# RWKV's 64x64 blocks all turned by products with the identity, none in TensorE's transpose mode

## The chip, the cores and the metric

The kernel runs on one core of one Trainium2 chip. The metric is device time in microseconds (us) of one execution, lower is better. The engines named are TensorE (PE, with its weight loads PEld), VectorE (DVE), ScalarE (ACT), GpSimd (POOL) and SyncE (SP, which issues most DMAs).

## What is computed

One inference step of a two-layer decoder for 256 prompt positions and 8 sample rows, so that each activation tile has 264 columns. Layer 0 runs an RWKV-7 mixer and an S5 mixer side by side, layer 1 a retention mixer; each layer ends with a SwiGLU FFN. The part that this change touches is RWKV's recurrence over the prompt, for 16 heads of width 64:

```python
def step(S, inp):
    r_t, w_t, k_t, v_t, kk_t, a_t = inp
    sa = jnp.einsum('bhij,bhj->bhi', S, kk_t)
    S = (S * w_t[:, :, None, :] - sa[..., None] * (kk_t * a_t)[:, :, None, :]
         + v_t[..., None] * k_t[:, :, None, :])
    return S, jnp.einsum('bhij,bhj->bhi', S, r_t)
```

The kernel computes it in 4 chunks of 64 positions for a pair of heads at a time. In that form blocks of 64x64 (values, scores, and matrices of a step-wise inversion) are needed turned, rows for columns.

## The kernel before

All weights stream from HBM in loads of 512 KB. ACT rounds each 128x512 piece to `wh`, DVE forms the rest `wl`, and PE multiplies three times (`xh,wh`, `xl,wh`, `xh,wl`) for float32 accuracy. `run_stream` writes these stream products in one fixed order: layer 0's input projection, a GLU, its output projection, the FFN, then layer 1.

RWKV, S5 and the eight sample rows are side work. Each is a generator that records operations; `pump` puts recorded operations between stream products, at most 3.3 us of PE work by its own count for a set of four weight blocks in layer 0. What is ready is judged by a planner's clocks: `emit` adds the price of each operation from `cost`. No wait that the chip really has comes back into it, and on each engine the instructions then run in exactly the order written. For PE the prices (us, at full clock; doubled when the planner thinks the clock low) of the 64x64 work are:

```python
            if name == "transpose":
                return 0.11 if w > 64 else 0.04
            if w <= 32:
                return max(0.034, 0.02 + 0.42e-3 * n)
            if w <= 64:
                return max(0.08, 1.05e-3 * n)
```

RWKV's prompt part handles head pairs p = 0 to 7. `front(p)` prepares a pair and `back(p)` does the chunked recurrence. `HS` are the two halves of the 128 partitions, one head in each, `NC_` is 4 chunks, `id2` an identity in each half. `turned` turns one block. It is called in four groups for each pair: in `front` eight times for the values `xv` (from one half into the other), and in `back`, at level 0, eight times for the scores `at`, six times for `AR` (chunks 1 to 3) and eight times for `Ym`. Within a group the output goes to the upper and the lower half in turn. In the trace a block in transpose mode leaves one MATMUL record, a float32 product leaves two.

The sample rows (`rwkv_sample_half`) matter because they wait for DMAs. For each of the eight pairs DVE multiplies a product with `bones` (a 128x512 multiply that reads `ps`), POOL subtracts, a DMA spreads a row over 64 partitions, and then DVE multiplies again, `self.mul(t, t, vb("k"))`, a 128x512 multiply that waits for that DMA. All that stands behind it on DVE waits with it, the `wl` pieces of the stream too.

Of the kernel before, what the change touches and what calls it, by code (L numbers as in the profile page):

```python
# [41 lines left out]
FAR = 1 << 20  # L42
# [85 lines left out]
class Builder:  # L128
# [271 lines left out]

    def turned(self, out, a, one):

        if out.offset % FAR < out.ap[0][0]:
            self.P.transpose(out, a, one)
        else:
            self.P.matmul(out, a, one, start=True, stop=True)

    def gcopy(self, out, a):
        self.G.tensor_scalar(out, a, 1.0, None, op0=OP.mult)
# [1399 lines left out]
```

## Time and profile before

| what | value |
|---|---|
| median of 3 runs (lowest, highest) | 3212.47 us (3202.04, 3217.61) |
| the profiled execution's own time | 3204.68 us |
| its span, first to last instruction | 3202.9 us |
| busy PE, DVE, ACT, POOL | 3121.3 us, 1972.0 us, 1498.7 us, 343.4 us |
| mean granted TensorE clock | 0.981 |
| first load of FFN weights issued at | 719.2 us |

RWKV's prompt part, where the change lies, runs between some 80 and 650 us from the span's start; behind it PE runs stream products almost without a gap. A MATMUL record's length is not what it costs, since records overlap; what counts is the distance from one start to the next.

### The profile page before, as it was taken

How to read it: one execution, taken by the hardware profiler on the slowest of the kernel's cores; microseconds unless marked ns; L12 is line 12 of the kernel's file. 1: busy time of each engine (PE TensorE's matmuls, PEld its weight loads, DVE VectorE, ACT ScalarE, POOL GpSimd, SP SyncE). 2: the span in 40 equal slices, each digit the busy share in tenths (PEclk: the TensorE clock that was granted, in tenths of full speed). 3: DMA queues.
4: the chain of work that ended last, by engine and by line, in shares of the span. 5: the costliest groups of instructions: out<-in, count | busy, mean ns of one | idle time of the engine just before them, and what ended most of it. 6: DMA issues, size and time to landing. Idle time of an engine off the chain costs nothing.

```text
span 3202.9 us, 65844 instructions
## 1 busy us (share of the span) xinstructions
PE 3121.3 (97%) x26390; PEld 2967.3 (93%) x26390; DVE 1972.0 (62%) x3702; ACT 1498.7 (47%) x2733; POOL 343.4 (11%) x525
## 2 busy tenths in 40 slices
PE   7999798899999999999999999999999999999998
PEld 7987687799999999999998998988899999999998
DVE  6788666466555555566566666565566565555554
ACT  6543355255444444455344444444455444444454
POOL 5111332100000000001111111011100000000001
PEclk9999899799999999999999999999999999999999
DMA  5323413455655556666666677567666555565654
GB/s 192 120 86 74 61 54 70 84 163 183 179 184 180 182 179 184 181 182 211 216 230 219 230 250 254 174 244 250 217 179 184 181 182 184 178 183 180 184 179 152
DMA packets 161138, 560.54 MB, mean 175 GB/s; under 512 B 21312, under 2 KB 23744, under 8 KB 160576
## 3 DMA queue, kind: packets, MB, share of 16 engines
q1 hardware_dynamic: 140384, 483.29, 50.7%
q0 software_dynamic: 19584, 71.31, 5.9%
q8 instruction: 207, 3.39, 0.4%
q10 hardware_dynamic: 864, 1.74, 0.1%
q14 instruction: 99, 0.81, 0.1%
HBM read 511.45 MB, written 42.69 MB: 173 GB/s over the span
## 4 chain that ended last, share of the span: by engine, by line
PE 92%; DVE 3%; DMA 2%; ACT 1%; POOL 1%; issue 0%; SPq 0%; DVEq 0%; POOLq 0%; ACTq 0%
PE ps L279 92%; DMA ar_tmp<-ar_tmp 2%; DVE ar_tmp L279 1%; POOL ar_tmp L279 1%; DVE wl L279 1%; DVE t L279 1%; ACT ar_tmp L279 0%; ACT wh L279 0%; DVE ar_hidb L279 0%; DVE ar_hidy L279 0%; SPq L279 0%; DVE xl L279 0%; DVE ar_hida L279 0%; POOL ar_hida L279 0%; ACT L285 0%
## 5 line engine op out<-in xcount | busy, mean ns | idle before, releaser
L279 DVE TENSOR_TENSOR wl<-raw,wh 128x512 fp32r<-128x512 f32 x1784 | 1260.6, 710 | 904.1 <-ACT wh L279 892.5
L279 ACT ACTIVATE wh<-raw 128x512 fp32r<-128x512 f32 x1784 | 1098.9, 628 | 936.3 <-PE ps L279 905.5
L279 PE MATMUL ps<-xh,wh 128*128 128x264 f32 x4512 | 1330.0, 295 | 14.7 <-ACT wh L279 12.4
L279 PE MATMUL ps<-xh,wl 128*128 128x264 f32 x4512 | 1289.7, 286 | 10.8 <-DVE wl L279 10.7
L279 PE MATMUL ps<-xl,wh 128*128 128x264 f32 x4512 | 1287.8, 285 | 0.0
L279 PEld LDWEIGHTS ps<-xh,wh 128*128 128x128 f32 x4512 | 858.8, 190 | 63.4 <-issue 28.6
L279 PEld LDWEIGHTS ps<-xh,wl 128*128 128x128 f32 x4512 | 856.4, 190 | 12.6 <-DVE wl L279 12.6
L279 PEld LDWEIGHTS ps<-xl,wh 128*128 128x128 f32 x4512 | 860.0, 191 | 5.7 <-issue 4.8
L279 PE MATMUL ps<-hl,wh 128*128 128x264 f32 x1280 | 364.0, 284 | 0.0
L279 PE MATMUL ps<-hh,wl 128*128 128x264 f32 x1280 | 363.9, 284 | 0.0
L279 PE MATMUL ps<-hh,wh 128*128 128x264 f32 x1280 | 363.8, 284 | 0.0
L279 PE MATMUL ps<-n,wh 128*128 128x264 f32 x1408 | 257.4, 284 | 0.0
L279 PE MATMUL ps<-ar_tmp 64*64 64x64 f32 (+8 forms) x2912 | 215.3, 283 | 39.5 <-DVE ar_tmp L279 24.6
L279 PEld LDWEIGHTS ps<-hh,wh 128*128 128x128 f32 x1280 | 241.4, 189 | 0.0
L279 PEld LDWEIGHTS ps<-hl,wh 128*128 128x128 f32 x1280 | 240.9, 188 | 0.0
L279 PEld LDWEIGHTS ps<-hh,wl 128*128 128x128 f32 x1280 | 240.7, 188 | 0.0
L279 PEld LDWEIGHTS ps<-ar_tmp 64*64 64x64 f32 (+3 forms) x2912 | 149.3, 149 | 82.3 <-DVE ar_tmp L279 28.9
L279 POOL TENSOR_TENSOR sqs<-sq,sqs 128x264 f32<-128x264 f32 x56 | 42.4, 758 | 1663.5 <-ACT sq L279 1663.5
L279 PEld LDWEIGHTS ps<-n,wh 128*128 128x128 f32 x1408 | 217.8, 188 | 0.0
L279 PE MATMUL ps<-n,wl 128*128 128x264 f32 x704 | 199.6, 284 | 0.0
L279 PE MATMUL ps<-omh,wh 128*128 128x264 f32 x512 | 147.1, 287 | 0.0
L279 PE MATMUL ps<-omh,wl 128*128 128x264 f32 x512 | 145.6, 284 | 0.0
(214 smaller groups left out, 2872.1 us busy)
## 6 DMA issues: line engine op xcount, KB each, us to landing
raw<-in_w_in_c_dram SPq DMA_DIRECT2D x192, 512.0 KB, 4.3
raw<-in_ffn_w_gate_dram SPq DMA_DIRECT2D x176, 512.0 KB, 3.6
raw<-in_ffn_w_up_dram SPq DMA_DIRECT2D x176, 512.0 KB, 3.7
raw<-in_ffn_w_down_dram SPq DMA_DIRECT2D x176, 512.0 KB, 3.7
out_dram<-ar_tmp POOLq DMA_DIRECT2D x72, 512.0 KB, 4.3
raw<-in_w_in_a_dram SPq DMA_DIRECT2D x68, 512.0 KB, 3.7
ar_tmp<-in_state_ret_dram POOLq DMA_DIRECT2D x64, 512.0 KB, 6.9
raw<-in_w_out_c_dram SPq DMA_DIRECT2D x64, 512.0 KB, 3.8
```

The costliest lines, as they stand in the source:

```text
L279: getattr(eng.eng, name)(*a, **k)
```

## The change

`turned` no longer looks at where its output lies. Before, a block whose output starts at partition 0 went through `P.transpose` and one whose output starts at partition 64 through `P.matmul` with the identity; now both go through `P.matmul`. Numbers are the same up to rounding.

```diff
     def turned(self, out, a, one):
 
-        if out.offset % FAR < out.ap[0][0]:
-            self.P.transpose(out, a, one)
-        else:
-            self.P.matmul(out, a, one, start=True, stop=True)
+        self.P.matmul(out, a, one, start=True, stop=True)
```

The planner now prices such a block 0.08 instead of 0.04, so that what `pump` places around it moves. The number of instructions on each engine stays: 21546 rows on PE, 2665 rows on DVE, before and now.

On PE, at the level-0 groups of an early pair: `cst` is the identity's tile, the group of six is `AR`, the group of eight behind it is `at`, and `xh,wh` and the like are stream products. Before:

```order
L279 MATMUL ps_76<-xh,wl 128x264
L279 MATMUL ps_71<-cst,ar_hidb 128x128 x4
L279 MATMUL ps_70<-cst,ar_hidb 64x64 x6
L279 MATMUL ps_72<-cst,ar_tmp 64x64 x8
L279 MATMUL ps_76<-xh,wh 128x264
L279 MATMUL ps_76<-xl,wh 128x264
```

Now, at the same place:

```order
L279 MATMUL ps_75<-xh,wl 128x264
L279 MATMUL ps_71<-cst,ar_hidb 128x128 x4
L279 MATMUL ps_70<-cst,ar_hidb 64x64 x6
L279 MATMUL ps_72<-cst,ar_tmp 64x64 x8
L279 MATMUL ps_71<-ar_tmp 64x64 x8
L279 MATMUL ps_75<-xh,wh 128x264
```

The groups themselves stay as they are; a group of score products (`ar_tmp 64x64 x8`) now follows at once, ahead of the stream products.

On DVE, in the second half of the sample rows: the first row is the multiply of the `bones` product, the last is the multiply that waits for the DMA, `wl<-raw,wh` is a piece of the stream, the rest is RWKV's. Before, all rows between the two:

```order
L279 TENSOR_TENSOR ar_tmp<-ps_72,ar_tmp 128x512
L279 TENSOR_TENSOR wl<-raw,wh 128x512
L279 TENSOR_TENSOR ar_tmp<-ps_71,cst 128x256
L279 TENSOR_TENSOR ar_tmp<-ar_tmp,ps_70 128x256
L279 TENSOR_TENSOR ar_hidb<-t_77,ar_hida 128x4x64
L279 TENSOR_TENSOR ar_tmp<-ar_tmp,ps_72 128x256
L279 SCALAR_TENSOR_TENSOR ar_hidy<-t_77,pcol,ar_hidy 128x256
L279 TENSOR_TENSOR ar_tmp<-ar_tmp,ps_69 128x256
L279 TENSOR_TENSOR ar_hidb<-ar_hidy,ar_hida 128x4x64
L279 SCALAR_TENSOR_TENSOR ar_hidy<-t_77,pcol,ar_hida 128x256
L279 TENSOR_TENSOR ar_tmp<-ar_tmp 128x512
```

Now, the last twelve rows up to the waiting multiply (four more stand between the first multiply and these):

```order
L279 TENSOR_TENSOR ar_tmp<-ar_tmp,ps_69 128x256
L279 TENSOR_TENSOR ar_hidb<-ar_hidy,ar_hida 128x4x64
L279 TENSOR_TENSOR ar_hidb<-cst,ps_71 128x3x64
L279 SCALAR_TENSOR_TENSOR ar_hidy<-t_77,pcol,ar_hida 128x256
L279 TENSOR_TENSOR ar_hidb<-ar_hidy,ar_hida 64x4x64
L279 TENSOR_TENSOR wl<-raw,wh 128x512
L279 TENSOR_TENSOR ar_hidb<-ar_hidy,ar_hida 64x4x64
L279 TENSOR_TENSOR ar_hidb<-ar_hidb,ps_72 128x3x64
L279 TENSOR_TENSOR ar_tmp<-ps_70,ar_hidx 128x256
L279 TENSOR_TENSOR ar_tmp<-ps_69,cst 128x256
L279 TENSOR_TENSOR ar_hidb<-ps_71,t_77 128x256
L279 TENSOR_TENSOR ar_tmp<-ar_tmp 128x512
```

The waiting multiply came 10 rows after the first multiply and now comes 15 rows after it. Over the eight pairs of the sample rows these distances were 18, 13, 14, 11, 10, 8, 9 and 8 rows (91 in all) and are now 19, 14, 20, 20, 15, 9, 10 and 6 (113 in all).

## Rows read from the trace of the kernel before

**Rows 1.** The page: the chain that ended last, shares by engine.

```profile
PE 92%; DVE 3%; DMA 2%; ACT 1%; POOL 1%; issue 0%; SPq 0%; DVEq 0%; POOLq 0%; ACTq 0%
```

**Rows 2.** Busy time of each engine (instructions) in stretches from the span's start.

```profile
core 0: us, PE busy (x) PEld busy (x) DVE busy (x) ACT busy (x) POOL busy (x), PEclk, DMA share, GB/s
...
160.00:240.00 80.00, 75.20 (x761) 65.03 (x761) 67.69 (x189) 33.60 (x67) 12.97 (x25) 0.94 0.28 85
240.00:320.00 80.00, 73.61 (x834) 61.25 (x830) 67.29 (x205) 26.06 (x55) 15.52 (x23) 0.91 0.35 75
...
720.00:800.00 80.00, 79.83 (x657) 79.56 (x657) 49.52 (x85) 43.46 (x81) 3.79 (x5) 1.00 0.60 181
80.00:640.00 560.00, 510.21 (x5459) 437.61 (x5458) 392.20 (x1024) 235.79 (x518) 132.90 (x211) 0.91 0.35 78
```

**Rows 3.** Pieces of the chain: start us, us, what; xn merges n pieces.

```profile
242.20 35.31 PE ps L279 x465
...
293.02 10.07 DMA ar_tmp<-ar_tmp
...
371.75 10.56 DMA ar_tmp<-ar_tmp
...
578.78 10.08 DMA ar_tmp<-ar_tmp
```

**Rows 4.** Waits, 80 to 660 us: who <- for whom: us, times, longest.

```profile
DVE ar_tmp L279 <- DMA ar_tmp<-ar_tmp: 50.0, 8, 9.1
...
PE ps L279 <- DVE ar_tmp L279: 28.4, 12, 7.3
```

**Rows 5.** PE's timeline, one group of eight turned blocks: start us, us, xrecords.

```profile
187.05 0.24 PE L279 MATMUL ps<-cst,ar_tmp 64*64 64x64 f32 x1
...
187.22 0.27 PE L279 MATMUL ps<-cst,ar_tmp 64*64 64x64 f32 x1
...
187.05 1.78 PE L279 MATMUL ps<-cst,ar_tmp 64*64 64x64 f32 x12
188.76 0.39 PE L279 MATMUL ps<-xh,wh 128*128 128x264 f32 x1
```

**Rows 6.** PE's timeline, groups of eight and of six 64x64 products alone.

```profile
425.99 0.68 PE L279 MATMUL ps<-ar_tmp 64*64 64x64 f32 x16
426.60 0.70 PE L279 MATMUL ps<-ar_tmp,cst 128*128 128x256 f32 x2
...
259.57 0.56 PE L279 MATMUL ps<-ar_hidb,ar_tmp 64*64 64x64 f32 x12
260.07 0.72 PE L279 MATMUL ps<-ar_hidx,ar_hida 64*128 64x264 f32 x4
```

**Rows 7.** PE's timeline, a turned group in DVE's wait for a DMA.

```profile
372.37 1.78 PE L279 MATMUL ps<-cst,ar_tmp 64*64 64x64 f32 x12
```

**Rows 8.** Both kinds of group while the clock was low; windows as in rows 2.

```profile
599.88 2.64 PE L279 MATMUL ps<-cst,ar_tmp 64*64 64x64 f32 x12
602.45 1.22 PE L279 MATMUL ps<-ar_tmp,cst 128*128 128x256 f32 x2
...
304.43 1.12 PE L279 MATMUL ps<-ar_tmp 64*64 64x64 f32 x16 [5.19 <-DVE ar_tmp L279]
305.48 0.79 PE L279 MATMUL ps<-ar_hidy,cst 128*128 128x256 f32 x1
...
301.00:315.00 14.00, 10.57 (x75) 7.45 (x76) 9.66 (x25) 0.00 (x0) 4.45 (x8) 0.51 0.30 83
...
591.00:615.00 24.00, 22.65 (x181) 17.20 (x180) 10.62 (x24) 7.26 (x16) 4.71 (x5) 0.51 0.55 89
```

**Rows 9.** DVE's timeline up to a multiply that waits for its DMA.

```profile
289.28 0.68 DVE L279 TENSOR_TENSOR ar_tmp<-ps,ar_tmp 128x512 f32<-128x512 f32 x1
...
296.97 0.26 DVE L279 TENSOR_TENSOR t<-t,ar_tmp 128x64 f32<-128x64 f32 x1
303.18 0.69 DVE L279 TENSOR_TENSOR ar_tmp<-ar_tmp 128x512 f32<-128x512 f32 x1 [5.95 <-DMA ar_tmp<-ar_tmp]
```

## The prediction

> **What bounds the kernel now.** I read the chain that ended last first: 92% of it is PE, with only 3% DVE and 2% DMA [rows 1]. The table by stage then shows where that is not the whole story. From 640 us on PE has nothing to wait for (79.83 us busy in a stretch of 80), while between 80 and 640 us, the stage of RWKV's prompt part, PE is busy for 510 of 560 us at a granted clock of 0.91, and DVE comes close behind with 67.7 and 67.3 us busy in stretches of 80 [rows 2]. In this stage the chain alternates: long PE pieces such as the one of 35.31 us from 242 us, then DVE pieces, and seven DMA pieces of some 10.5 us each, of which three are shown [rows 3]. The list of waits says whose they are: DVE waits for the sample rows' DMA eight times, 50.0 us in all, and PE in turn waits 28.4 us for what DVE makes [rows 4]. So a microsecond saved on PE in this stage counts where the chain is PE, and is lost where a DMA or DVE would have come last anyway.
>
> **What a turned group costs now.** Eight blocks, four in transpose mode and four as products, leave 4 x 1 + 4 x 2 = 12 records. One such group starts at 187.05 us and the next instruction behind it at 188.76 us: 1.71 us, or 0.43 us for a pair of one transposition and one product. Within the pair the transposition's start is 0.17 us ahead of the product's first pass (187.05 to 187.22), so the product takes the other 0.26 us until the next transposition begins [rows 5]. Nothing in the group overlaps.
>
> **What it will cost.** The trace has the new form already: groups of eight float32 products of 64x64, alternating between the same two halves. Eight products are 16 records and take 425.99 to 426.60 = 0.61 us; six products are 12 records and take 259.57 to 260.07 = 0.50 us [rows 6]. More records take about a third of the time because products for the two halves run side by side. The bounds: at best 0.61 us a group, at worst, if products with the identity don't overlap, 8 x 0.26 = 2.08 us. I take 0.61 us, since shape, halves and alternation are those of the rows; `front`'s group crosses from one half to the other, which also gives two different halves in turn.
>
> There are 8 head pairs x 4 groups = 32 groups, 24 of eight blocks and 8 of six. The saving for a group of eight is 1.71 - 0.61 = 1.10 us, for one of six 3 x 0.43 - 0.50 = 0.79 us. PE's saving is 24 x 1.10 + 8 x 0.79 = 32.7 us.
>
> **What of it lies on the path.** I laid the starts of the 32 groups beside the chain's pieces. Six lie outside its PE pieces: four in DMA pieces, as the one at 372.37 us in the piece from 371.75 [rows 3, 7], and two ahead of the piece at 293 us, where DVE leads. Five are of eight blocks and one of six. The other 26 (19 and 7) save 19 x 1.10 + 7 x 0.79 = 26.4 us.
>
> Three corrections.
>
> First, the clock. In 591 to 615 us the granted clock is 0.51, the level of 1.2 GHz, after PE had stood idle in the DMA waits before it. Three groups lie there. At this level a mixed group takes 599.88 to 602.45 = 2.57 us and a group of products, in a stretch of the same clock, 304.43 to 305.48 = 1.05 us: 1.52 instead of 1.10 us saved, so 3 x 0.42 = 1.3 us more [rows 8].
>
> Second, DVE. Eleven of the 26 groups (8 and 3) start before 280 us, where DVE is busy for 67 of 80 us [rows 2]. They save 8 x 1.10 + 3 x 0.79 = 11.2 us; with PE that much quicker DVE has little slack left and will sometimes be last instead. Between nothing and all of it lost, I take half: 5.6 us.
>
> Third, the order that moved. The multiply that waits for the sample rows' DMA now stands 113 rows behind the first multiplies, over the eight pairs, where it stood 91. In the trace the 18 rows of the first pair take DVE from 289.28 to 297.23 us, of which 0.4 us is idle, 0.42 us a row, and only then does it wait 5.95 us [rows 9]. 22 rows more are 22 x 0.42 = 9.2 us of work done in the shadow that DVE waited through. Part of it would have been hidden elsewhere; between 0 and 9.2 I take half, 4.6 us. Had the order moved the other way, by 22 rows less, it would cost the same. No DMA, no wait and no instruction is added on any engine.
>
> The sum: 26.4 + 1.3 - 5.6 + 4.6 = 26.7 us. From the profiled execution's 3204.7 us that gives 3178.0 us. The median of the three runs is 7.8 us above the profiled execution, so I forecast 3212.5 - 26.7, rounded to 3186 us, for the median. The runs of before spread over 15.6 us, so 0.5%, 16 us, is about what can be told from no change.
>
> **A rule that speaks against it.** The row prices a transposition at 0.17 us and a product at 0.26 us in the mixed group [rows 5]. The Trainium skill, "TensorE: Matmul & The Clock Gate", section "Terms", says of the transpose mode that it is four times faster for float32. By that rule a transposition would take an estimated quarter of 0.26 us, 0.065 us, and the change would add 120 x 0.195 = 23 us, to 3236 us. The trace does not agree: the start-to-start distance is 0.17 us. I give this 0.01, inside the 0.04 of the second rival below.
>
> **Rivals.**
>
> *The saving is swallowed in the stage.* PE reaches the waits of [rows 4] earlier and stays in them longer, and before 400 us DVE and the DMA chain alone set the pace. Then only the groups after 400 us count, 11 of eight and 4 of six: 11 x 1.10 + 4 x 0.79 + 1.3 = 16.6 us, and with half of it lost again 8 us. For it speaks DVE's 67 us in 80; against it that PE pieces between 113 and 277 us still lead the chain, as the one of 35.31 us [rows 3]. Time: 3212.5 - 8 to 16, about 3200 us.
>
> *Passes, not switching, are what a turned block costs.* Twelve records take 1.71 us, 0.143 us each [rows 5]. If every pass with the identity costs that, 120 blocks with one pass more make 120 x 0.143 = 17 us more on PE, 3230 us. With products that merely don't overlap it is 24 x (2.08 - 1.71) + 8 x (6 x 0.26 - 1.29) = 11 us more, 3224 us. It decides as soon as a group of eight takes over 1.71 us. Against it speak the groups in [rows 6], 0.61 us for 16 records.
>
> *The DMA waits come out.* With a shorter PE and another order each DMA piece could leave PE idle for longer. PE's waits for DVE would have to grow from 28.4 us by 27 + 16 = 43 us before the kernel were slower by 0.5%. The order moved the other way (113 rows for 91), so I give it little.
>
> **How the numbers follow.** The forecast, a gain of over 16 us with the likeliest at 26.7 us: 0.74. Swallowed, 8 to 16 us: 0.20. Passes or no overlap: 0.04, half of it over 0.5% slower. DMA waits come out: 0.02. So faster by over 0.5% 0.74, within 0.5% 0.22, slower 0.04. The range: at its low end all 32 groups count, DVE takes nothing and the order gives its 9.2 us: 32.7 + 1.3 + 9.2 = 43 us, 3169 us; a draw of runs near the lowest of before, 10 us under the median, could add to that, and I go to 3165. At its high end stands the swallowed saving with 8 us, 3204 us, and I go to 3206. Of the forecast alone the range is 3168 to 3197 us.
>
> **What would show it.** Right: each group of eight turned blocks has 16 records and takes about 0.61 us, PE has 120 more records than before, the first load of FFN weights is issued near 692 us instead of 719.2, and behind it stretches of 80 us look as before; DVE's eight waits for the sample's DMA fall from 50.0 towards 41 to 46 us. Wrong: groups of 16 records that take over 1.2 us would show that products with the identity don't overlap; groups of 0.61 us with a first FFN load still after 705 us would show that the stage's waits took the saving, and PE's waits for DVE would then be well over 28 us.

## The result and the profile after

Four runs of the changed kernel took 3173.37 to 3177.85 us, median 3176.42; the kernel before took 3202.04 to 3217.61 us beside them, median 3211.47. The ratio is 0.9892 with a 95% interval of 0.9867 to 0.9918: faster by 1.1%, 35 us by the medians. The profiled executions lie 27.9 us apart (3204.68 and 3176.80 us), their spans 28.0 us (3202.9 and 3174.9). The difference between 35 and 28 us is scatter of the kernel before, whose profiled execution is among its quick ones: its 26 executions on record took 3202.0 to 3221.9 us. What is read from spans and traces below holds for the profiled executions, so the medians are given beside them.

PE's timeline after, one group of eight turned blocks, with the instruction behind it; it answers to [rows 5]:

```profile
184.69 0.68 PE L279 MATMUL ps<-cst,ar_tmp 64*64 64x64 f32 x16
185.30 0.39 PE L279 MATMUL ps<-xh,wh 128*128 128x264 f32 x1
```

Sixteen records from 184.69 to 185.30, 0.61 us where twelve took 1.71. At the lower clock too the group takes what products took there before, 1.05 us (554.00 to 555.05), and not 2.57 [rows 8]. Two such rows of PE's timeline after, and the stretch around them in the table by stage, where PEclk, the third figure from the end, is the granted clock:

```profile
554.00 1.12 PE L279 MATMUL ps<-cst,ar_tmp 64*64 64x64 f32 x16
555.05 0.59 PE L279 MATMUL ps<-xh,wh 128*128 128x264 f32 x1
```

```profile
549.00:557.00 8.00, 8.00 (x83) 6.82 (x84) 4.58 (x12) 1.51 (x4) 1.78 (x2) 0.50 0.40 138
```

The first FFN load marks the end of the stage. It was issued at 719.2 us and now is at 691.2, 28.0 us earlier, the whole difference of the spans:

```profile
L279 SPq DMA_DIRECT2D raw<-in_ffn_w_gate_dram x176: 327/328/328, 691.2 to 3017.4; - x176
```

So the stage from 80 us to this load can be taken by itself. Its row in the table by stage, first of before, then of after (the columns are those of [rows 2]):

```profile
80.00:719.20 639.20, 589.41 (x6159) 515.08 (x6159) 445.47 (x1125) 275.79 (x597) 140.44 (x221) 0.92 0.37 89
```

```profile
80.00:691.20 611.20, 550.27 (x6267) 488.59 (x6267) 439.44 (x1122) 274.89 (x598) 139.49 (x221) 0.93 0.39 92
```

PE is busy for 39.1 us less (589.4 to 550.3) but idle for 11.1 us more (639.2 - 589.4 = 49.8, then 611.2 - 550.3 = 60.9). That is the reading to take with you: length = busy + idle, and the idle part gave back over a quarter of what the busy part saved. The waits of after say where, beside [rows 4]:

```profile
DVE ar_tmp L279 <- DMA ar_tmp<-ar_tmp: 49.3, 8, 7.9
```

```profile
PE ps L279 <- DVE ar_tmp L279: 39.8, 19, 6.7
```

DVE waits for the sample rows' DMA as long as before (49.3 against 50.0 us), where I had foretold 41 to 46 us, and PE waits for DVE 39.8 instead of 28.4 us.

### The profile page after: what moved, and what is told of

It is laid out like the page before. It is cut to its first block, busy times and chain, and to the rows that moved or that the text cites. A ratio compares the mean times of both kernels' runs of the same rounds, so it can differ in the third digit from the quotient of the medians.

```text
span 3174.9 us, 66100 instructions
## 1 busy us (share of the span) xinstructions
PE 3083.1 (97%) x26510; PEld 2941.5 (93%) x26510; DVE 1965.8 (62%) x3701; ACT 1498.3 (47%) x2734; POOL 341.6 (11%) x525
## 4 chain that ended last, share of the span: by engine, by line
PE 89%; DVE 4%; DMA 3%; ACT 2%; POOL 2%; issue 1%; SPq 0%; DVEq 0%; POOLq 0%; ACTq 0%
PE ps L279 89%; DMA ar_tmp<-ar_tmp 2%; DVE ar_tmp L279 2%; DVE wl L279 1%; DVE t L279 1%; ACT ar_tmp L279 1%; POOL ar_tmp L279 1%; ACT wh L279 0%; DVE ar_hida L279 0%; POOL sq L279 0%; DMA out_dram<-ar_tmp 0%; ACT t L279 0%; SPq L279 0%; POOL t L279 0%; POOL rstd L279 0%
## 5 line engine op out<-in xcount | busy, mean ns | idle before, releaser
L279 PE MATMUL ps<-xh,wh 128*128 128x264 f32 x4512 | 1326.3, 294 | 16.1 <-ACT wh L279 12.4
L279 PE MATMUL ps<-xh,wl 128*128 128x264 f32 x4512 | 1287.6, 285 | 10.1 <-DVE wl L279 10.0
L279 PEld LDWEIGHTS ps<-xh,wh 128*128 128x128 f32 x4512 | 855.7, 190 | 64.3 <-issue 27.8
```

The lines of the kernel that those rows point to most:

```text
L279: getattr(eng.eng, name)(*a, **k)
```

## The experiments

Two questions were open. Is it the engine's saving or the new order of the instructions that brought the 28 us? And where did the rest of PE's saving go? "Span" below is always of the profiled execution (3202.9 before, 3174.9 after). For every run the stage from 80 us to the first FFN load is split as above. The medians are those of all executions of a kernel; beside them before had medians of 3211.47 us (after), 3217.47 (e1 to e4), 3219.29 (e5 to e8) and 3215.97 (e9 to e11), and the ratios are to these.

| run | span | stage | PE busy | PE idle | median of runs | ratio of runs to before (95%) |
|---|---|---|---|---|---|---|
| before | 3202.9 | 639.2 | 589.4 | 49.8 | 3211.47 to 3219.29 | |
| after | 3174.9 | 611.2 | 550.3 | 60.9 | 3176.42 | 0.9892 (0.9867 to 0.9918) |
| e1, old order, products | 3185.7 | 622.0 | 553.3 | 68.7 | 3187.25 | 0.9908 (0.9890 to 0.9926) |
| e2, new order, half transposed | 3192.2 | 628.5 | 579.3 | 49.2 | 3200.60 | 0.9949 (0.9930 to 0.9968) |
| e3, before, sorted by half | 3190.4 | 626.8 | 566.5 | 60.3 | 3193.37 | 0.9929 (0.9914 to 0.9944) |
| e4, after, sorted by half | 3172.6 | 609.0 | 552.5 | 56.5 | 3174.67 | 0.9871 (0.9856 to 0.9886) |
| e6, before, no spreading DMA | 3148.4 | 584.2 | 570.0 | 14.2 | 3146.33 | 0.9780 (0.9757 to 0.9802) |
| e7, e1, no spreading DMA | 3117.4 | 553.3 | 525.4 | 27.9 | 3118.54 | 0.9693 (0.9673 to 0.9714) |
| e9, before, DMA planned at 10 us | 3155.5 | 591.9 | 570.0 | 21.9 | 3158.26 | 0.9828 (0.9802 to 0.9855) |
| e5, after, DMA planned at 10 us | 3116.3 | 552.6 | 526.1 | 26.5 | 3118.52 | 0.9692 (0.9667 to 0.9717) |

**e1: products in the old order.** The planner prices as before; only what is written to PE changes, in `emit`:

```diff
+        if name == "transpose" and a[1].shape[0] == 64:
+            name, k = "matmul", dict(start=True, stop=True)
         getattr(eng.eng, name)(*a, **k)
```

> Every instruction stands where it stood before the change (the planner still prices these blocks as transpositions), but all turned blocks run as products. Theory 1 (the saving is PE's own, because transposition and product in turn don't overlap): a group of eight takes 0.61 us instead of 1.71, the 32 groups about 19 us instead of 52, and the span falls by 22 to 33 us from 3202.9. Rival (the new order of the instructions brings the gain): the span stays within 8 us of before, whatever the groups take.

The span fell by 17.2 us, short of the 22 to 33 us of theory 1 and more than the rival's 8. The medians lie further apart, by 30.2 us (3217.47 to 3187.25), and the interval of the ratio allows 24 to 35 us. By either measure PE's own saving is the larger part of the gain; how much of it arrives depends on which executions of before are taken. Stage and waits of e1:

```profile
80.00:702.00 622.00, 553.31 (x6279) 492.22 (x6277) 444.37 (x1125) 275.08 (x597) 143.18 (x221) 0.92 0.38 91
```

```profile
DVE ar_tmp L281 <- DMA ar_tmp<-ar_tmp: 56.1, 8, 9.1
```

```profile
PE ps L281 <- DVE ar_tmp L281: 40.8, 19, 7.3
```

PE is busy for 36.1 us less and idle for 18.9 us more. DVE, which gets to the DMAs sooner, waits 6.1 us longer for them (50.0 to 56.1), and PE's wait for DVE grows by 12.4 us (28.4 to 40.8).

**e2: the new order alone.** The prices of after, the instructions of before:

```diff
+        if "turn" in k:
+            name, k = ("transpose", {}) if k["turn"] else (name, dict(start=True, stop=True))
         getattr(eng.eng, name)(*a, **k)
```

(`turned` passes `turn` where the output starts at partition 0.)

> The order of the changed kernel with the turned blocks as before, half of them in transpose mode: the order alone. Theory 1: groups of eight take 1.71 us and the span is within 8 us of before's 3202.9 us; my third correction put the order alone at 0 to 9 us gained. Rival (the order brings the gain): the span is near the changed kernel's 3175 us.

The span fell by 10.7 us, a little more than either allowed for the order alone. Together with e1's 17.2 us it makes 27.9, the 28.0 us of the whole change. That the two parts add is not shown, though: by the medians they are 30.2 and 16.9 us, 47 in all, where the whole change is 35 us by its own median of before and 41 by this one. Among kernels with products alone, whose executions lie close together, the order is worth 10.8 us by spans and by medians alike (e1 to after). In e2 the order did not work as I had it. Its stage and DVE's wait:

```profile
80.00:708.50 628.50, 579.34 (x6150) 505.02 (x6149) 438.56 (x1122) 275.10 (x598) 139.49 (x221) 0.93 0.38 90
```

```profile
DVE ar_tmp L281 <- DMA ar_tmp<-ar_tmp: 48.3, 8, 7.9
```

DVE's wait for the DMA is only 1.7 us shorter, and PE's idle time is the same (49.2 against 49.8). What fell is PE's busy time, by 10.1 us with the same instructions; the granted clock of the stage rose from 0.92 to 0.93. Less of the same work fell into stretches at the lower clock. This holds for these two executions; whether the order brought the higher clock is not shown by them, since the four executions of e2 themselves were granted 0.978 to 0.985.

**e3 and e4: groups sorted by half.** All blocks of one half first, then those of the other, in before (four transpositions, then four products) and in after (eight products that share halves with their neighbours):

```diff
-            for c in range(c0, NC_):
-                for h in range(2):
+            order = [(h, c) for c in range(c0, NC_) for h in range(2)]
+            if len(f(0, c0)) == 1:
+                order.sort()
+            for h, c in order:
```

and the two loops of `front`'s group exchanged.

> The kernel before, with the blocks of a group sorted: first the four in transpose mode, then the four products, so that a group switches once and not seven times. Theory 1 (it is the switching back and forth that costs): the group falls from 1.71 us to about 1.0 to 1.2 us, and the span by 8 to 20 us. Rival (a transposition costs 0.17 us and a product 0.26 us by themselves): the group stays at 1.7 us and the span within 5 us of before.

PE's timeline of e3:

```profile
183.67 1.01 PE L279 MATMUL ps<-cst,ar_tmp 64*64 64x64 f32 x12
184.62 0.39 PE L279 MATMUL ps<-xh,wh 128*128 128x264 f32 x1
```

The same four transpositions and four products take 0.95 us instead of 1.71 once they are sorted, so it is the going back and forth between the two that costs: 0.76 us for six switches fewer, 0.13 us each. In the mixed group each switch is also a change of half, but e4 shows below that changing halves among products costs nothing: it gains. Within the sorted group a transposition starts 0.056 us after the one before it, and a product takes 0.117 us (single records between 183.75 and 184.47 us). So the 0.17 and 0.26 us of the mixed group are mostly not the blocks' own [rows 5]. The span fell by 12.5 us, the median by 24.1. The rival is out.

> The changed kernel with the products of a group sorted by half, so that neighbours share a half. Theory 1 with overlap of the two halves as the reason for 0.61 us: without it the group takes 16 passes of about 0.054 us and an end, some 1.0 us, and the span rises by 8 to 14 us over the changed kernel's 3174.9. Rival (no overlap of halves is needed, products are cheap back to back): the group stays at 0.61 to 0.7 us and the span within 4 us.

```profile
182.98 0.96 PE L279 MATMUL ps<-cst,ar_tmp 64*64 64x64 f32 x16
183.88 0.39 PE L279 MATMUL ps<-xh,wh 128*128 128x264 f32 x1
```

The group takes 0.90 us instead of 0.61: running the two halves side by side is worth 0.29 us a group, somewhat less than I expected, and the rival's 0.61 to 0.7 us is out. But the span did not rise by 8 to 14 us; it is 2.3 us lower than the changed kernel's. Some 9 us more work in 32 groups (32 x 0.29, a little less for the groups of six) did not lengthen the stage: PE is busy for only 2.2 us more, at a granted clock of 0.985 over the span instead of 0.983, and idle for 4.4 us less. So 1.71 to 0.61 splits into about 0.8 us from having no switches and 0.3 us from the halves, and the stage did not feel the last part.

**e6 and e7: the waits taken away.** Before and e1, in their unchanged order, without the sixteen DMAs that spread sample values over partitions. This leaves out a part of the sample rows' state update, so only the time counts.

```diff
+        spread = key == "D" and a[0].shape[0] == 64 and all(type(x.tensor).__name__ == "Tile" for x in a[:2])
...
-        getattr(eng.eng, name)(*a, **k)
+        if not spread:
+            getattr(eng.eng, name)(*a, **k)
```

> The kernel before, all instructions in their order, but without the sixteen DMAs that spread the sample rows' values over the partitions: this leaves out part of the sample rows' state update and is there for its time alone. Both theories: the DMA waits of 50.0 us go, and the span falls by 30 to 50 us from 3202.9. It is the partner of the next run.

> The same without the sixteen DMAs (so without that part of the sample rows' update), with all turned blocks as products in the old order. What counts is its distance to the run before it in this list. Theory 1 (the DMA waits gave back half of PE's 34 us): without them the products save 26 to 34 us instead of the 17 us that they saved in the old order with the waits. Rival (DVE's work gave it back): again 14 to 20 us.

The pair, e6 first:

```profile
80.00:664.20 584.20, 569.95 (x6155) 498.62 (x6154) 442.17 (x1125) 275.87 (x597) 141.76 (x221) 0.96 0.31 93
```

```profile
80.00:633.30 553.30, 525.40 (x6275) 469.63 (x6274) 442.60 (x1125) 275.06 (x597) 143.68 (x221) 0.98 0.33 99
```

The span of e6 fell by 54.5 us, somewhat beyond the 30 to 50 expected. PE runs the instructions of before in their order and is idle for 35.6 us less (49.8 to 14.2), but also busy for 19.4 us less (589.4 to 570.0), at a clock of 0.96 instead of 0.92. The waits had cost PE twice: as idle time and as work done at the lower clock.

Between e6 and e7 the products save 31.0 us of span, against 17.2 us for the same edit in the same order with the DMAs in place. That the waits on these DMAs took the difference, as theory 1 has it, is not shown. By the medians the products save 27.8 us without the DMAs (3146.33 to 3118.54) and 30.2 with them. In the profiled executions the 13.8 us of difference have two parts. PE's idle time rises by 13.7 us without the DMAs and by 18.9 with them, so that 5.2 us go with the waits on DMAs and most of what is given back does not. PE's busy time falls by 44.6 us instead of 36.1, more than the groups themselves, as the clock goes from 0.96 to 0.98, where before and e1 both have 0.92. Whether that step in the clock comes of the missing DMAs or of scatter is open: the executions of e6 were granted 0.990 to 0.992 over the span, and the profiled one is the longest of them.

So the rival is not out either: with no such DMA at all PE still waits longer for what DVE makes, in short waits. e6, then e7:

```profile
PE ps L281 <- DVE ar_tmp L281: 5.1, 8, 1.6
```

```profile
PE ps L283 <- DVE ar_tmp L283: 11.0, 15, 1.9
```

The stretch from 80 us to the first multiply of the sample rows, ahead of all these DMA waits, shows the same. Before, e1, e6, e7:

```profile
80.00:289.30 209.30, 201.68 (x1990) 181.79 (x1990) 176.85 (x492) 98.22 (x199) 32.37 (x59) 0.97 0.32 97
```

```profile
80.00:279.50 199.50, 187.56 (x2043) 172.78 (x2041) 175.84 (x491) 97.75 (x199) 32.75 (x59) 0.97 0.33 102
```

```profile
80.00:288.20 208.20, 200.60 (x1985) 180.57 (x1984) 176.84 (x491) 98.25 (x199) 32.59 (x59) 0.97 0.32 97
```

```profile
80.00:278.70 198.70, 186.76 (x2039) 171.81 (x2038) 176.11 (x491) 97.79 (x199) 32.87 (x59) 0.97 0.34 102
```

The products shorten it by 9.8 us with the DMAs and by 9.5 without them, and PE's idle time grows from 7.6 to 11.9 us in both pairs.

**e5 and e9: the waits planned around.** After and before, with the planner told what the DMA takes; nothing is left out:

```diff
+        if spread:
+            t = max(t + 10.0, self.clk["D"]) + c
-        if key == "D":
+        elif key == "D":
             t = self.clk["D"] = max(t + 1.7, self.clk["D"]) + c
```

> The changed kernel, but the planner counts the sample rows' spreading DMA as landing 10 us after its issue (about what the trace shows) and not 1.7 us, so that the waiting multiply stands 20 to 39 rows behind the first multiply instead of 6 to 20. Theory 1 (half of PE's saving was given back in the waits that these DMAs cause): DVE's eight waits fall from 49.3 us to under 20 us, PE's idle time in the stage falls, and the kernel gains another 15 to 35 us, to 3140 to 3160 us. Rival (DVE's own work is the bound that took the saving): DVE's waits move elsewhere and the time stays within 8 us of the changed kernel's 3176 us.

DVE's wait in e5, and its stage:

```profile
DVE ar_tmp L282 <- DMA ar_tmp<-ar_tmp: 1.1, 1, 1.1
```

```profile
80.00:632.60 552.60, 526.13 (x6277) 471.19 (x6275) 440.79 (x1116) 278.73 (x606) 140.20 (x221) 0.98 0.43 103
```

The wait is down from 49.3 to 1.1 us, and the span from 3174.9 to 3116.3 us, more than theory 1 asked. Of these 58.6 us PE's idle time gives 34.4 and its busy time 24.2, as the clock of the stage goes from 0.93 to 0.98: the waits cost twice here too. The median of 3118.52 us makes this the quickest of all complete kernels here.

> The kernel before (half of the turned blocks in transpose mode, priced as before), with the planner counting the spreading DMA as 10 us. With its partner, the changed kernel with the same planner (3118.5 us, span 3116.3), it tells what the change is worth where the DMA waits are planned around. Theory 1 (the waits took half of PE's saving): the change is worth 24 to 36 us there, so that this kernel takes 3142 to 3155 us. Rival (PE's saving is carried by half in any case): 14 to 20 us, 3132 to 3139 us.

With the same planner and the turned groups of before the span is 3155.5 us. The change is worth 39.2 us here (39.7 by the medians), beyond theory 1's 36, where it was worth 28 us by spans and 35 by medians without this planning. These two kernels differ in order as well, so that not all of it need be the engine's, and how much the covered waits add is not settled by this pair.

**e8, e10, e11: other prices, other orders.** The changed kernel with the planner's price of a turned block at 0.06, 0.10 and 0.07:

```diff
+            if name == "turn":
+                return 0.06
```

> The changed kernel with the planner's price of a turned block between the two, 0.06: another order of the same instructions. If the 10.7 us that the new order alone brought come from a price nearer to what such a block costs, the time lies between those of the two orders with products, 3176 and 3187 us. If they are a matter of how pieces happen to fall, it can lie as well outside, by up to 15 us either way.

This one told nothing of orders: 2 x 0.06 is what the pair cost before (0.04 + 0.08), and the order came out as that of e1. It is a repetition of e1, and its span of 3185.4 us (3185.7) shows how well spans of this kernel repeat; those of before do not.

> The changed kernel with the planner's price of a turned block at 0.10 instead of 0.08: a third order of the same instructions (the price of 0.06 turned out to give the order of before). The distance of the waiting multiply is 92 rows in all, where before had 91 and the changed kernel 113. If the new order's 10.7 us hang on that distance, the span is near 3186 us; if a price of at least what the block costs brings them, near 3175 us; if they are how pieces happen to fall, it can be anything from 3165 to 3195 us.

> The same with the price at 0.07: a fourth order, with 96 rows. If the distance of the waiting multiply decides: near 3185 us. If the price does, nearer to what a block costs being better (0.61 us over eight is 0.076 us): near 3175 us. If it is how pieces fall: anything from 3165 to 3195 us.

| order of | rows to the waiting multiply | DVE's wait for the DMA | span |
|---|---|---|---|
| e1 (and e8) | 91 | 56.1 | 3185.7 |
| e10 | 92 | 55.9 | 3185.0 |
| e11 | 96 | 53.2 | 3186.0 |
| after | 113 | 49.3 | 3174.9 |

All four run products throughout. Three orders with 91 to 96 rows lie within 1 us; the price as such does not decide. The order of after stands alone with 113 rows, 4 to 7 us less waiting and 11 us less time. That fits the distance as the cause but rests on one order with a long distance (and on e5, with 20 to 39 rows at each of the eight places and hardly any waiting); in the profiled execution of e2 the same order gained by the clock instead. e8's ratio to before was 0.9906 (0.9885 to 0.9927), e10's 0.9924 (0.9899 to 0.9949), e11's 0.9918 (0.9892 to 0.9943). How much of the 11 us is the distance and how much chance stays open.

## Why the prediction came out right

**The price of a group** was right: 1.71 us before, 0.61 us after, and 1.05 us at the low clock. That eight products with the identity would run like any other products, bounds of 0.61 and 2.08 us, was the main choice, and it held. PE's busy time in the old order fell by 36.1 us (e1), against the 32.7 + 1.3 = 34.0 us worked out. The reason given was only half right. I put the third of the time down to the halves running side by side; e3 and e4 show that this is about 0.3 us of the 1.1, and that having no switches is the other 0.8. The split of a pair into 0.17 us for the transposition and 0.26 us for the product [rows 5] took the cost of switching for the blocks' own.

**What of it arrives.** I had 26.4 + 1.3 on the path less 5.6 us for DVE, 22.1 us. e1 measured 17.2 by spans and 30.2 by medians, so the record does not say whether the sum was too high. In the profiled executions its parts were off. Up to the first multiply of the sample rows 9.8 us arrived, where I had left 5.6 (11.2 less half): PE did wait longer for DVE, but by 4.3 us only. Behind it 17.2 - 9.8 = 7.4 us arrived, where I had 15.2 + 1.3 = 16.5: PE's idle time grew by 14.6 us there, and my sum had nothing for that. Laying groups beside the chain says what lies on it before, not how far it can shrink until a wait takes over. Most of the waits that grew are not the DMAs', as the 13.7 us of e6 and e7 show.

**The order** was too low: 4.6 us against 10.8 with products (e1 to after). The work in DVE's shadow fits there, with 56.1 to 49.3 us of waiting, but against before as a whole DVE's wait did not fall to the 41 to 46 us that I had named. With transpositions the gain of the profiled execution, 10.7 us, lay in the clock (e2).

By spans the misses nearly cancel: 22.1 + 4.6 = 26.7 us foretold, 17.2 + 10.7 = 27.9 us measured. So the first FFN load came at 691.2 us, where I had named 692, and that closeness is partly luck. The forecast of 3186 us was 10 us above the median of 3176.42, inside the range; most of that is the step from the profiled execution to a median of before, 7.8 us, which I added and the changed kernel doesn't have.

**The rivals.** "Swallowed in the stage" names a mechanism that is there: in e1's profiled execution PE's idle time took 18.9 us back of 36.1, and PE's waits for DVE reached 39.8 us in after, the sign that I had named for it. But the first FFN load came well before 705 us, and the groups ahead of 400 us did count. "Passes, not switching" fell with the group's 0.61 us, and e3 adds that the same records in another order take 0.95 us instead of 1.71. "The DMA waits come out": PE's waits for DVE grew by 11.4 us, far from the 43 us needed. The rule of the Trainium skill in "TensorE: Matmul & The Clock Gate", section "Terms", that transpose mode is four times faster for float32, gave an estimated loss of 23 us; the trace does not agree for this mix, where a mixed group takes 1.71 us and a group of products 0.61. Without the switches, in e3's sorted group, a transposition is about twice as quick as a product (0.056 against 0.117 us).

## What to carry to other kernels

Alternating a cheap operation with another kind can cost more than using the dearer kind throughout: read the distance between starts in the very mix that runs, beside a group of the same shape that runs pure. Then ask what PE will wait for once it is quicker: here idle time took back 11.1 us of the 39.1 us that its busy time lost, mostly in waits for DVE. A wait on the busiest engine can cost twice, as idle time and as work at the lower clock behind it, so that a planner that is told the true length of one transfer gained 58.6 us of span (e5 over after), where the change itself gained 28.0. And set single traces beside the medians before one difference of spans is held against another: 17.2 against 31.0 us by spans (e1, and e7 against e6) was 30.2 against 27.8 by medians.

## What I had not expected of the hardware

- Going from transpose mode to products and back costs PE about 0.13 us a switch (e3: six switches fewer, 0.76 us less).
- Kernels with mixed groups scatter more from run to run: over 19.8 us for before in all its runs (3202.0 to 3221.9), 10.2 for e2, 7.6 for e6 and 4.9 for e9. Those with products alone stay within 1.2 us (e7) to 6.5 us (e10), after within 4.5, and e3, with its sorted groups, within 2.0. In before the time goes with the granted clock: executions at 0.981 took 3202 to 3207 us and those at 0.976 3219 to 3222 us, and 0.005 of 3200 us is 16 us. Why one kernel is granted different clocks is open.
- The same instructions in another order made PE busy for 10.1 us less in the profiled execution (e2), with the granted clock of the stage at 0.93 instead of 0.92. In before's order without sixteen DMAs they made it busy for 19.4 us less, at 0.96 (e6).
